# A two-block network: the mixer's projections in another order, its modulation columns made earlier and later

## The chip, the cores and the metric

One program runs on one core of one Trainium2 chip. The metric is the time of one execution on the device, in microseconds (us). The kernel before took 1466.2 us (median of three runs, 1460.26 to 1466.62).

The core has a matrix engine (PE; PEld is its loading of weights), a vector engine (DVE), an activation engine (ACT), a general engine (POOL) and SP, which here does nothing but start DMA transfers, one after the other, in the order in which they are written. Each engine takes its own instructions in order, and waits for the others by semaphores.

## The reference, cut to what matters

Two blocks run one after the other on 256 tokens of width 1024, in float32. The first has two layers of attention and mlp, the second a mixer and a mixture of 16 experts. Before each of these parts the input is normed and modulated by a shift and a scale, and its result is added through a gate. These six columns of 1024 numbers come from a conditioning vector by a matrix product of its own:

```python
mod = cond @ ada_w[layer] + ada_b[layer]                       # first block, per layer
sh1, sc1, g1, sh2, sc2, g2 = jnp.split(mod, 6, axis=-1)
...
m  = jax.nn.silu(c) @ w_mod[l] + b_mod[l]                      # second block
mc = jax.nn.silu(c_ctx) @ w_mod[l] + b_mod[l]                  # the same for its context of 256 tokens
h  = rms_norm_2(x, norm1_g[l]) * (1.0 + sc1) + sh1
hc = rms_norm_2(xc, norm1_g[l]) * (1.0 + csc1) + csh1
...
gq, gk, gv, nq, nk, nv, fu, cu, gl = jnp.split(h @ w_in, ...)  # the mixer
y_gqa = gqa_latent(q, k, v, kc, vc)                            # grouped-query attention
y_na  = neighbourhood_latent(nq, nk, nv, nkc, nvc, rpb)        # neighbourhood attention
y_fn  = fourier_mix(fu)
y_cv  = conformer_conv(cu, ...)     # a * sigmoid(b), 31 taps along the tokens, norm, silu
out   = merge_branches((y_gqa, y_na, y_fn, y_cv), gl, w_branch, w_out)
x = x + g1 * y                      # then norm, sh2, sc2, the experts, g2
```

## The kernel before

Every product of float32 matrices is made of three products of a reduced kind: a tile of 128 x 1024 weights (512 KB) is brought by DMA into `raw`; ACT casts it to `hi` (L322), DVE subtracts to get `lo` (L323), and PE multiplies hi by hi, hi by lo and lo by hi (`mm3`, L334 to L336). `raw` has four buffers, `hi` and `lo` five each. A tile of weights that DVE or ACT splits late holds PE.

The modulation columns are not made on PE. A step of `gemv_steps` brings a 512 KB tile of `adaT` into `ada` (two buffers) and has DVE multiply it by the conditioning row, which lies in a `crow` tile, and sum it into one of 48 columns of `mod` (L461). Steps are queued with `later` or `todo`, and `fill(n)` makes the next n of them wherever the program calls it. There are 128 such loads. `mod[0]` and `mod[1]` belong to the two layers of the first block, `mod[2]` to the second block; `modc` holds the first 16 columns for the context.

The order is this. The second attention, `odd`, has projections, the difference attention (scores L671, their row maximum on DVE at L673, values L1279) and, threaded into it, MoBA attention with its output projection at the end; it makes no columns. The second mlp, `mlp(1)`, goes through eight steps `c`; each has 96 matmuls of 256 columns for w1 (L1195 to L1197) and 48 of 512 for w2, and calls `fill(FILL[1][c])`: first the eight columns 40 to 48 of `mod[1]` (its own gate), then the conditioning rows of the second block (`silu_row`), and its columns 0 to 16, with two DVE instructions each since `modc` is made from the same tile. `block2_rows` is the queue of the second block.

The mixer projects the keys, values and queries of grouped-query attention; then `others()` yields step by step through the neighbourhood keys (`nkT`) and values (`nv`), the two halves of the convolution's input (`za`, `z`), the neighbourhood queries (`nqT`) and Fourier's input (`u`). The attention's loop `attend(gqa, ...)` takes a step of `others()`, `FILL_GQA` columns and `EARLY_CONV` steps of the convolution at each of its yields: scores on PE (L1465), their maximum on DVE (`nm`, L1467), the exponential on ACT, a transpose and a copy (`row`, L651), the values (L1437). A convolution is 4 x 30 taps, each one DVE instruction (L1539), plus four first ones (L1535). `attend(na, ...)` does the same for the neighbourhood attention (L1482, L1487), with `CONV` steps of the convolution and the merges of the other branches beside it. Last come `merge(1)`, the output projection and the routing to experts.

Slots (`A1`, `A2`, `O0`, `O1`) are named places in the memory; a tile that takes a slot waits until its last holder has been read. The list that each engine works through comes from a scheduler, which places instructions by its own estimates within the written order.

Of the kernel before, what the change touches and what calls it, by code (L numbers as in the profile page):

```python
# [27 lines left out]
ODD_COLS = [(512 * i, 512 * i + 512) for i in range(6)]  # L28
FILL = [[6] * 8, [4, 4, 4, 4, 4, 4, 0, 0]]
LAST_T = 4  # L30
# [7 lines left out]
NRAW = 12  # L38
CONV = 3
TAPS = 3  # L40
EARLY_CONV = 1
NATIVE = ("raw", "hi", "lo") * 4 + ("hi", "lo")
# [19 lines left out]
CONTEXT = [0] * 6 + [2, 2]  # L62
FILL_GQA = [3,2,2,1,2,2,2,1,2,2,2,2,0,2,2,0,4]
FILL_NA = []
# [17 lines left out]
def pack(w, us):  # L82
# [13 lines left out]
    + [GQ + 64 * h + d for h in range(8) for d in HALF]  # L96
    + list(range(NK, NK + 512)) + list(range(NV, NV + 512))
    + list(range(CU, CU + 1024)) + list(range(NQ, NQ + 512)) + list(range(FU, FU + 512))
    + [GL + D * n + c for n in MERGE for c in range(D)]
# [147 lines left out]
class Block:  # L247
# [900 lines left out]
    def mlp(self, l):  # L1148
# [4 lines left out]
        acc = [[self.ps(tag="pj"), self.ps(tag="pj")], [self.ps(tag="pj"), self.ps(tag="po")]]  # L1153
        self.later(l, [self.crow0], [mod], range(40, 48))
        if l == 0:
            for a, b in ((0, 16), (16, 24), (24, 40)):
                self.later(1, [self.crow0], [self.mod[1]], range(a, b))
        else:
            self.todo.append(self.block2_rows())
            context = self.context()  # L1160
# [60 lines left out]
    def block2_rows(self):  # L1221

        mod = self.mod[2]
        cc, c2 = self.silu_row(2), self.silu_row(1)
        yield from self.gemv_steps(2, [cc, c2], [self.modc, mod], range(0, 16))
        for a, b in ((16, 24), (24, 40), (40, 48)):
            yield from self.gemv_steps(2, [c2], [mod], range(a, b))

    def odd(self):
# [22 lines left out]
        def val(v):  # L1252
            def g(t, ps, w):
                nc.scalar.copy(v[:, t], ps)
            yield from self.native_steps(st, self.hf, g)
# [66 lines left out]
        def side():  # L1322
# [3 lines left out]
            yield from moba  # L1326

        for g in (qk_(("diff_q_norm", "diff_k_norm"), q1), val(v1)):
            for _ in g:
                pass  # L1330
        side = side()
        for _ in difference_whole():
            next(side, None)
        out = self.out_proj(Stream(A["odd_out"], units(D, COLS_1024, 0)), 8, oT)
        for _ in moba:
# [48 lines left out]
    def mixer(self):  # L1384
# [108 lines left out]
        nkT = self.slot("A1", [P, 4, 512])  # L1493
        nv = self.slot("A2", [P, 4, 512])
        zz = self.slot("O0", [P, 2, 4, S])
        z, za = zz[:, 0], zz[:, 1]
        u = self.slot("O1", [P, 2, 512])

        def others():

            def f(n, ps):
                nc.scalar.copy(nkT[:, n], ps)
            yield from self.proj_T(st, [h, hc], f, 1)

            def f(i, ps, w):
                nc.scalar.copy(nv[:, i], ps)
            yield from self.proj_steps(st, D, four, f)

# [11 lines left out]

            def f(n, ps):
                nc.scalar.mul(nqT[:, n], ps, 0.125)
            yield from self.proj_T(st, [h], f, 2)

            def f(t, ps, w):
                nc.scalar.copy(u[:, t], ps)
            yield from self.proj_steps(st, D, acts, f)
# [27 lines left out]
        for _ in side:  # L1555
            pass


# [79 lines left out]
        for g in (cv, side):  # L1638
            for _ in g:
                pass  # L1640
        self.fill(99)
        mT = (self.slot("A1", [P, 8, S], F32R), self.slot("A2", [P, 8, S], F32R))
        for _ in merge(1, y1):
            pass
        for i, y in enumerate((y0, y1, y2)):
# [461 lines left out]
```

## Time and profile before

| | |
|---|---|
| median of three runs | 1466.2 us |
| the profiled execution, its own time | 1464.86 us |
| its span (first to last instruction) | 1463.1 us |
| mean granted TensorE clock | 0.969 |
| PE busy | 1379.0 us, 94% |
| PEld busy | 1115.6 us, 76% |
| DVE busy | 1111.6 us, 76% |
| ACT busy | 817.0 us, 56% |

The parts that the change touches lie, in us from the span's start, at about 409 to 547 (`odd`), 547 to 760 (`mlp(1)`), 760 to 812 (first projections of the mixer), 812 to 907 (grouped-query attention with `others()`), 907 to 930 (Fourier), 930 to 1046 (neighbourhood attention with merges) and 1046 to 1105 (`merge(1)` and the output projection). The share of a busy engine over the whole span says little about one of these; each is read for itself.

### The profile page before, as it was taken

Reading aid. Unit: us, or ns where it says so; the run is one execution under the profiler, and the core shown is the slowest. Engines: PE = TensorE matmul, PEld = TensorE weight load, DVE = VectorE, ACT = ScalarE, POOL = GpSimd, SP = SyncE. Lnnn points to the kernel's source line nnn. Section 1 sums busy time; section 2 is a strip of 40 time slices with the busy share of each in tenths; the row PEclk is TensorE's granted clock in tenths of the full one; section 3 lists DMA queues with packets and bytes.
Section 4 is the critical chain, followed back from the end, with each engine's and each line's share of the span. In section 5 each row is a group of like instructions: output and inputs, shape, how many; then the busy total and the mean of one; then the engine's idle time right before and its main releaser. Section 6 shows DMA issues by size and latency. Waiting matters only on the chain.

```text
span 1463.1 us, 20532 instructions
## 1 busy us (share of the span) xinstructions
PE 1379.0 (94%) x7366; PEld 1115.6 (76%) x7366; DVE 1111.6 (76%) x1879; ACT 817.0 (56%) x1304; POOL 153.6 (11%) x189
## 2 busy tenths in 40 slices
PE   6879899999999999999999999999998899999996
PEld 4768668989854557989988897677786788888884
DVE  4779777778753666799775679997676888888986
ACT  4456455445422455545655556555545487778764
POOL 0269410000022200000003000000000000000001
PEclk9999799999999979999999999999999899999998
DMA  9657447899972222878633777444554599999993
GB/s 350 242 187 235 159 153 241 304 312 316 333 250 85 101 88 98 304 255 295 241 126 122 238 239 233 143 144 147 177 188 157 185 344 341 328 334 324 331 330 142
DMA packets 93838, 333.56 MB, mean 228 GB/s; under 512 B 10656, under 2 KB 11808, under 8 KB 93216
## 3 DMA queue, kind: packets, MB, share of 16 engines
q1 hardware_dynamic: 93728, 332.17, 66.1%
q8 instruction: 60, 0.98, 0.3%
q14 instruction: 50, 0.41, 0.1%
HBM read 331.08 MB, written 1.05 MB: 227 GB/s over the span
## 4 chain that ended last, share of the span: by engine, by line
PE 65%; DMA 12%; DVE 11%; ACT 4%; issue 4%; POOL 3%; SPq 1%; ACTq 0%; POOLq 0%; DVEq 0%
PE pj L334 6%; PE pj L335 6%; PE pj L336 6%; DMA raw<-in_w_dram 6%; PE pj L381 5%; PE ps L334 5%; PE ps L336 5%; PE ps L335 5%; DMA ada<-in_adaT_dram 4%; PE ps L411 3%; DVE ada L461 3%; DVE lo L323 2%; ACT hi L322 2%; PE ps L1197 2%; PE ps L1195 2%
## 5 line engine op out<-in xcount | busy, mean ns | idle before, releaser
L322 ACT CAST hi<-raw 128x1024 fp32r<-128x1024 f32 (+3 forms) x311 | 313.2, 1016 | 235.5 <-DMA raw<-in_w_dram 84.6
L323 DVE TENSOR_TENSOR lo<-raw,hi 128x1024 fp32r<-128x1024 f32 (+4 forms) x301 | 357.7, 1198 | 98.6 <-ACT hi L322 95.8
L461 DVE CUSTOM_DVE_ANT_0 ada<-ada,crow 128x1024 f32<-128x1024 f32 x128 | 161.6, 1272 | 30.0 <-DMA ada<-in_adaT_dram 30.0
L334 PE MATMUL pj<-hi,H 128*128 128x512 f32 (+3 forms) x312 | 117.9, 382 | 3.7 <-ACT H L814 1.8
L1197 PE MATMUL ps<-H,lo 128*128 128x256 f32 x408 | 116.9, 286 | 2.3 <-DVE lo L323 2.2
L335 PE MATMUL pj<-lo,H 128*128 128x512 f32 (+3 forms) x312 | 117.0, 376 | 0.8 <-DVE lo L323 0.6
L334 PE MATMUL pj<-hi,A 128*128 128x512 f32 (+1 forms) x293 | 115.3, 394 | 2.4 <-DVE w L960 2.4
L1195 PE MATMUL ps<-H,hi 128*128 128x256 f32 x408 | 116.8, 286 | 0.7 <-ACT hi L322 0.7
L1196 PE MATMUL ps<-H,hi 128*128 128x256 f32 x408 | 116.3, 285 | 0.0
L335 PE MATMUL pj<-lo,A 128*128 128x512 f32 (+1 forms) x293 | 114.7, 392 | 0.7 <-DVE lo L323 0.6
L336 PE MATMUL pj<-hi,H 128*128 128x512 f32 (+3 forms) x312 | 115.2, 373 | 0.0
L336 PE MATMUL pj<-hi,A 128*128 128x512 f32 (+1 forms) x293 | 114.1, 389 | 0.0
L1197 PEld LDWEIGHTS ps<-H,lo 128*128 128x128 f32 x408 | 79.0, 194 | 3.2 <-DVE lo L323 3.1
L1195 PEld LDWEIGHTS ps<-H,hi 128*128 128x128 f32 x408 | 79.0, 194 | 1.6 <-ACT hi L322 0.9
L1196 PEld LDWEIGHTS ps<-H,hi 128*128 128x128 f32 x408 | 79.0, 194 | 0.4
L334 PEld LDWEIGHTS pj<-hi,H 128*128 128x128 f32 x312 | 59.7, 192 | 17.7 <-issue 6.0
L334 PE MATMUL ps<-hi,A 128*128 128x512 f32 x180 | 71.3, 396 | 0.0
L335 PE MATMUL ps<-lo,A 128*128 128x512 f32 x180 | 70.3, 391 | 0.0
L336 PE MATMUL ps<-hi,A 128*128 128x512 f32 x180 | 70.3, 391 | 0.0
L323 DVE TENSOR_TENSOR lo<-crow,hi 128x1024 fp32r<-128x1024 f32 x52 | 62.6, 1222 | 8.8 <-ACT hi L322 7.9
L334 PEld LDWEIGHTS pj<-hi,A 128*128 128x128 f32 x293 | 55.2, 189 | 16.3 <-issue 4.4
L335 PEld LDWEIGHTS pj<-lo,H 128*128 128x128 f32 x312 | 60.2, 193 | 9.3 <-DVE lo L323 1.1
(557 smaller groups left out, 3295.2 us busy)
## 6 DMA issues: line engine op xcount, KB each, us to landing
ada<-in_adaT_dram SPq DMA_DIRECT2D x128, 512.0 KB, 4.9
raw<-in_w_dram SPq DMA_DIRECT2D x128, 512.0 KB, 5.3
raw<-in_gu_dram SPq DMA_DIRECT2D x78, 512.0 KB, 5.7
raw<-in_in_dram SPq DMA_DIRECT2D x60, 512.0 KB, 4.3
raw<-in_down_dram SPq DMA_DIRECT2D x37, 512.0 KB, 5.5
crow<-in_gu_dram SPq DMA_DIRECT2D x34, 512.0 KB, 5.8
raw<-in_even_in_dram SPq DMA_DIRECT2D x24, 384.0 KB, 4.0
crow<-in_down_dram SPq DMA_DIRECT2D x18, 512.0 KB, 5.9
```

What stands on the lines that cost most here:

```text
L322: self.nc.scalar.copy(hi, src)
L323: end = (engine or self.nc.vector).tensor_tensor(lo, src, hi, ALU.subtract)
L334: mm(ps, ah, bh, start=start, stop=False)
L335: mm(ps, ah, bl, start=False, stop=False)
L336: mm(ps, al, bh, start=False, stop=stop)
L381: self.nc.tensor.matmul(pss[t], hf[:, k, t * P:t * P + P], ws[k], start=k == 0, stop=k == 7)
L411: self.nc.tensor.transpose(out, in_, self.ident[:p, :p])
L461: nc.vector.tensor_tensor_reduce(out=o, in0=wt, in1=r, scale=1.0, scalar=0.0, op0=ALU.mult, op1=ALU.add, accum_out=m[:, j:j + 1])
L1195: mm(ps[:, n % 2], wh, hh[:, k], start=k == 0 and n % 2 == 0, stop=False)
L1196: mm(ps[:, n % 2], wh, hl[:, k], start=False, stop=False)
L1197: mm(ps[:, n % 2], wl, hh[:, k], start=False, stop=k == 7 and n % 2 == 1)
```

## The change

The convolution's two projections come first in `others()`, ahead of the neighbourhood keys and values, and the weights' columns in `IN2_ORDER` move with them. `z` and `za` take the slot A2 (before: O0), `nv` takes O0 (before: A2), allocated when its first tile is copied; its four pieces come in another order, and the first is held in PSUM until the second is there. `u` is allocated later. `EARLY_CONV` is 2 (before: 1) and `CONV` is 1 (before: 3).

The columns of the modulation move. `odd` now makes 16: `mod[1]` 40 to 48, then, after the conditioning row, `mod[2]` 16 to 24, one at a time by `FILL_ODD`. `mlp(1)` makes 32 in all eight of its steps: 0 to 16 (with `modc`) from the first step on, then 24 to 40. The grouped-query attention makes none. The last eight, 40 to 48, are made in `merge(1)` by `FILL_MERGE`. Nothing else is computed than before, and 128 tiles of `adaT` are loaded as before.

```diff
-FILL = [[6] * 8, [4, 4, 4, 4, 4, 4, 0, 0]]
+FILL = [[6] * 8, [4, 4, 4, 4, 4, 4, 4, 4]]
+FILL_ODD = [0] + [1] * 20
-CONV = 3
+CONV = 1
-EARLY_CONV = 1
+EARLY_CONV = 2
-FILL_GQA = [3,2,2,1,2,2,2,1,2,2,2,2,0,2,2,0,4]
+FILL_GQA = []
+FILL_MERGE = [1, 1, 2, 1, 1, 2]
...
-    + list(range(NK, NK + 512)) + list(range(NV, NV + 512))
-    + list(range(CU, CU + 1024)) + list(range(NQ, NQ + 512)) + list(range(FU, FU + 512))
+    + list(range(CU, CU + 1024)) + list(range(NK, NK + 512)) + list(range(NV, NV + 512))
+    + list(range(NQ, NQ + 512)) + list(range(FU, FU + 512))
...
     def block2_rows(self):
         mod = self.mod[2]
-        cc, c2 = self.silu_row(2), self.silu_row(1)
-        yield from self.gemv_steps(2, [cc, c2], [self.modc, mod], range(0, 16))
-        for a, b in ((16, 24), (24, 40), (40, 48)):
-            yield from self.gemv_steps(2, [c2], [mod], range(a, b))
+        cc = self.silu_row(2)
+        yield from self.gemv_steps(2, [cc, self.c2], [self.modc, mod], range(0, 16))
+        for a, b in ((24, 40), (40, 48)):
+            yield from self.gemv_steps(2, [self.c2], [mod], range(a, b))
+
+    def odd_rows(self):
+        yield from self.gemv_steps(1, [self.crow0], [self.mod[1]], range(40, 48))
+        self.c2 = self.silu_row(1)
+        yield from self.gemv_steps(2, [self.c2], [self.mod[2]], range(16, 24))
...
+        fills = iter(FILL_ODD)
+        self.todo.append(self.odd_rows())
         for g in (qk_(("diff_q_norm", "diff_k_norm"), q1), val(v1)):
             for _ in g:
-                pass
+                self.fill(next(fills, 0))
         side = side()
         for _ in difference_whole():
             next(side, None)
+            self.fill(next(fills, 0))
+        self.fill(99)
...
-        nv = self.slot("A2", [P, 4, 512])
-        zz = self.slot("O0", [P, 2, 4, S])
+        zz = self.slot("A2", [P, 2, 4, S])
...
+            def f(i, ps, w):
+                held.append(ps)
+                if i:
+                    if not nvs:
+                        nvs.append(self.slot("O0", [P, 4, 512]))
+                    for n in range(len(held)):
+                        nc.scalar.copy(nvs[0][:, (i - len(held) + 1 + n + 2) % 4], held[n])
+                    held.clear()
...
-        self.fill(99)
         mT = (self.slot("A1", [P, 8, S], F32R), self.slot("A2", [P, 8, S], F32R))
-        for _ in merge(1, y1):
-            pass
+        fills = iter(FILL_MERGE)
+        for _ in merge(1, y1):
+            self.fill(next(fills, 0))
+        self.fill(99)
```

The scheduler's lists of the vector engine show what becomes of it at three places. The first is the end of the first mlp, where the second attention's norm begins: `w` (L887, L889 after) takes a result of the mlp out of PSUM, `x` adds it, the rows that write `A` make the normed input, and `rs` is its factor. Before:

```order
L887 TENSOR_TENSOR w_3891<-pj_2158,row_3778 128x512
L888 TENSOR_TENSOR x_12_80<-x_12_80,w_3891 128x512
L531 TENSOR_TENSOR A_780_3900<-x_12_80,row_3793 128x512
L887 TENSOR_TENSOR w_3895<-pj_2159,row_3778 128x512
L888 TENSOR_TENSOR x_12_80<-x_12_80,w_3895 128x512
L531 TENSOR_TENSOR A_780_3900<-x_12_80,row_3793 128x512
L507 SCALAR_TENSOR_TENSOR rs_3903<-ssx_79,rs_3903 128x1
L539 SCALAR_TENSOR_TENSOR A_780_3900<-A_780_3900,rs_3903,xn_3806 128x512
```

After:

```order
L889 TENSOR_TENSOR w_3891<-pj_2158,row_3778 128x512
L890 TENSOR_TENSOR x_12_80<-x_12_80,w_3891 128x512
L533 TENSOR_TENSOR A_780_3900<-x_12_80,row_3793 128x512
L463 ISA ada_4023,mod_2_62<-ada_4023,crow_461 128x1024
L463 ISA mod_2_62 128x1
L889 TENSOR_TENSOR w_3895<-pj_2159,row_3778 128x512
L890 TENSOR_TENSOR x_12_80<-x_12_80,w_3895 128x512
L533 TENSOR_TENSOR A_780_3900<-x_12_80,row_3793 128x512
L463 ISA ada_4077,mod_2_62<-ada_4077,crow_461 128x1024
L463 ISA mod_2_62 128x1
L509 SCALAR_TENSOR_TENSOR rs_3903<-ssx_79,rs_3903 128x1
L541 SCALAR_TENSOR_TENSOR A_780_3900<-A_780_3900,rs_3903,xn_3806 128x512
```

Two modulation columns (L463, before L461) stand now ahead of `rs`.

The second place is the first step of the second mlp on the same engine, where `lo` are splits of its weights and `modc_64` the context's columns. Before:

```order
L323 TENSOR_TENSOR A_1047_5006<-ps_5007,A_1047_5006 128x4x128
L461 ISA ada_5014,mod_2_62<-ada_5014,crow_461 128x1024
L461 ISA mod_2_62 128x1
L461 ISA ada_5017,mod_2_62<-ada_5017,crow_461 128x1024
L461 ISA mod_2_62 128x1
L323 TENSOR_TENSOR lo_5169<-raw_5166,hi_5168 128x1024
L461 ISA ada_5020,mod_2_62<-ada_5020,crow_461 128x1024
L461 ISA mod_2_62 128x1
L323 TENSOR_TENSOR lo_5175<-raw_5172,hi_5174 128x1024
```

After:

```order
L325 TENSOR_TENSOR A_1065_5062<-ps_5063,A_1065_5062 128x4x128
L422 SCALAR_TENSOR_TENSOR crow_5070<-xn_5072,crow_5070 128x1024
L325 TENSOR_TENSOR lo_5239<-raw_5236,hi_5238 128x1024
L423 TENSOR_SCALAR crow_5070<-crow_5070 128x1024
L463 ISA xn_5078,modc_64<-ada_5076,crow_5070 128x1024
L463 ISA modc_64 128x1
L463 ISA ada_5076,mod_3_63<-ada_5076,crow_4357 128x1024
L463 ISA mod_3_63 128x1
L463 ISA xn_5083,modc_64<-ada_5081,crow_5070 128x1024
L463 ISA modc_64 128x1
L325 TENSOR_TENSOR A_1065_5062<-ps_5171,A_1065_5062 128x4x128
L463 ISA ada_5081,mod_3_63<-ada_5081,crow_4357 128x1024
```

Each tile of `adaT` is read twice from the first step on, and the conditioning row is made ahead of it.

The third place is the start of the grouped-query attention, again on the vector engine; `xn` is the low part of its second half of queries, `nm` the first row maximum. Before:

```order
L323 TENSOR_TENSOR lo_7472<-raw_7469,hi_7471 128x1024
L323 TENSOR_TENSOR xn_7416<-w_7157,xn_7416 128x8x64
L461 ISA ada_7442,mod_3_63<-ada_7442,crow_5462 128x1024
L461 ISA mod_3_63 128x1
L461 ISA ada_7445,mod_3_63<-ada_7445,crow_5462 128x1024
L461 ISA mod_3_63 128x1
L1467 TENSOR_REDUCE nm_7436<-ps_7433 128x1
```

After:

```order
L325 TENSOR_TENSOR lo_7571<-raw_7568,hi_7570 128x1024
L1520 SCALAR_TENSOR_TENSOR A_1443_7246<-w_7501,A_1443_7246 128x256
L1520 SCALAR_TENSOR_TENSOR A_1443_7246<-w_7504,A_1443_7246 128x256
L1560 SCALAR_TENSOR_TENSOR A_1443_7246<-A_1443_7246,cols_84 128x244
L325 TENSOR_TENSOR xn_7524<-w_7231,xn_7524 128x8x64
L1560 SCALAR_TENSOR_TENSOR A_1443_7246<-A_1443_7246,cols_84 128x245
L325 TENSOR_TENSOR lo_7863<-raw_7860,hi_7862 128x1024
L1560 SCALAR_TENSOR_TENSOR A_1443_7246<-A_1443_7246,cols_84 128x246
L1479 TENSOR_REDUCE nm_7544<-ps_7541 128x1
```

Convolution taps (L1560, before L1539) and the convolution's inputs (L1520) stand among the queries' splits and ahead of the maximum. All 120 taps lie ahead of the twelfth of the 16 maxima `nm`; before, 20 lay ahead of the fifteenth and the others behind it.

## Rows read from the trace of the kernel before

**Rows 1.** The page: engines by busy time, and the chain that ended last.

```profile
PE 1379.0 (94%) x7366; PEld 1115.6 (76%) x7366; DVE 1111.6 (76%) x1879; ACT 817.0 (56%) x1304; POOL 153.6 (11%) x189
...
PE 65%; DMA 12%; DVE 11%; ACT 4%; issue 4%; POOL 3%; SPq 1%; ACTq 0%; POOLq 0%; DVEq 0%
```

**Rows 2.** By stretch: PE, PEld, DVE, ACT, POOL busy, granted clock, DMA, GB/s.

```profile
812.00:907.00 95.00, 92.91 (x622) 79.98 (x621) 77.01 (x136) 52.23 (x93) 0.00 (x0) 1.00 0.73 244
...
930.00:1046.00 116.00, 114.93 (x564) 82.24 (x564) 97.60 (x231) 69.41 (x134) 1.86 (x2) 0.99 0.49 158
```

**Rows 3.** PE's waits from 760 to 1106: total, times, longest.

```profile
PE ps L1358 <- ACT pt L662: 1.5, 1, 1.5
PE ps L1482 <- DVE A L323: 1.1, 1, 1.1
...
PE ps L481 <- ACT row L482: 0.8, 1, 0.8
PE po L1437 <- DVE row L651: 0.6, 1, 0.6
```

**Rows 4.** PE in order of time, grouped-query attention: start, duration, what.

```profile
861.40 0.28 PE L1358 MATMUL ps<-H,hi 128*128 128x256 f32 x1
861.52 0.28 PE L1359 MATMUL ps<-H,hi 128*128 128x256 f32 x1
```

**Rows 5.** In order of time, start of the second attention, DVE and PE.

```profile
405.00 0.16 DVE L507 SCALAR_TENSOR_TENSOR rs<-ssx,rs 128x1 f32<-128x1 f32 x1
...
405.81 0.75 DVE L539 SCALAR_TENSOR_TENSOR A<-A,rs,xn 128x512 f32<-128x512 f32 x1 [0.66 <-POOL rs L508]
...
407.96 1.03 PE L411 MATMUL ps<-consts,A 128*128 128x128 f32 x8
...
409.77 1.98 PE L381 MATMUL pj<-hi,H 128*128 128x512 f32 x4 [0.77 <-ACT H L549]
```

**Rows 6.** In order of time, difference attention, DVE; then PE.

```profile
456.28 0.29 DVE L673 CUSTOM_DVE_ANT_0 sc<-ps,consts 128x128 f32<-128x128 f32 x1 [9.10 <-PE ps L671]
...
466.77 0.29 DVE L673 CUSTOM_DVE_ANT_0 sc<-ps,consts 128x128 f32<-128x128 f32 x1 [9.85 <-PE ps L671]
...
485.85 1.54 PE L1279 MATMUL po<-A,pt 128*128 128x128 f32 x6 [1.47 <-ACT pt L651]
```

**Rows 7.** Busy time by stretch, end of the second attention.

```profile
516.70:533.80 17.10, 16.53 (x54) 10.73 (x54) 9.56 (x31) 8.61 (x24) 2.41 (x4) 0.50 0.27 90
```

**Rows 8.** The tile `ada`, 540 to 1070: DVE's idle time for it, landing.

```profile
  DMA ada<-in_adaT_dram: 17.5, 19
...
DMA to landing us min/median/max: 3.2/4.8/8.5
```

**Rows 9.** Busy time by stretch in the second mlp; then PE's wait there.

```profile
600.00:620.00 20.00, 20.00 (x135) 18.54 (x134) 13.39 (x16) 9.12 (x12) 0.00 (x0) 1.00 0.90 309
620.00:640.00 20.00, 20.00 (x135) 18.54 (x134) 19.23 (x26) 11.91 (x15) 0.00 (x0) 1.00 0.71 234
...
PE ps L1197 <- DVE lo L323: 1.1, 1, 1.1
```

**Rows 10.** DVE's groups, 812 to 907; then 907 to 1046: busy, mean ns, idle.

```profile
L461 DVE CUSTOM_DVE_ANT_0 ada<-ada,crow 128x1024 f32<-128x1024 f32 x25 | 30.3, 1223 | 9.7 <-DMA ada<-in_adaT_dram 9.7
L323 DVE TENSOR_TENSOR lo<-raw,hi 128x1024 fp32r<-128x1024 f32 x20 | 24.2, 1220 | 2.1 <-ACT hi L322 2.1
L1467 DVE TENSOR_REDUCE nm<-ps 128x1 f32<-128x512 f32 x15 | 10.3, 686 | 2.3 <-PE ps L1465 2.3
...
L1539 DVE SCALAR_TENSOR_TENSOR O<-O,cols 128x251 f32<-128x251 f32 (+14 forms) x99 | 42.7, 470 | 0.0
```

**Rows 11.** In order of time, DVE: queries' low part, eight taps, `merge(1)`'s split.

```profile
810.85 0.69 DVE L323 TENSOR_TENSOR xn<-w,xn 128x512 fp32r<-128x512 f32 x1 [0.75 <-ACT xn L322]
...
920.32 3.18 DVE L1539 SCALAR_TENSOR_TENSOR O<-O,cols 128x245 f32<-128x245 f32 x8
...
1083.42 2.59 DVE L323 TENSOR_TENSOR lo<-raw,hi 128x1024 fp32r<-128x1024 f32 x2 [0.25 <-ACT hi L322]
```

More of the change, by code (lines that the diff above doesn't have):

```diff
@@ L1153, in mlp @@
         acc = [[self.ps(tag="pj"), self.ps(tag="pj")], [self.ps(tag="pj"), self.ps(tag="po")]]
-        self.later(l, [self.crow0], [mod], range(40, 48))
         if l == 0:
+            self.later(0, [self.crow0], [mod], range(40, 48))
             for a, b in ((0, 16), (16, 24), (24, 40)):
@@ L1493, in mixer @@
         nkT = self.slot("A1", [P, 4, 512])
-        nv = self.slot("A2", [P, 4, 512])
-        zz = self.slot("O0", [P, 2, 4, S])
+        zz = self.slot("A2", [P, 2, 4, S])
         z, za = zz[:, 0], zz[:, 1]
-        u = self.slot("O1", [P, 2, 512])
+        nvs, us = [], []
         def others():
[L1501 to L1507, printed above, removed]
             def f(n, ps):
@@ L1521, in f @@
             def f(n, ps):
+                nc.scalar.copy(nkT[:, n], ps)
+            yield from self.proj_T(st, [h, hc], f, 1)
+            def f(i, ps, w):
[6 more added lines that the diff above has]
+                    held.clear()
+            held = []
+            yield from self.proj_steps(st, D, four[2:] + four[:2], f)
+            def f(n, ps):
                 nc.scalar.mul(nqT[:, n], ps, 0.125)
             yield from self.proj_T(st, [h], f, 2)
+            us.append(self.slot("O1", [P, 2, 512]))
             def f(t, ps, w):
-                nc.scalar.copy(u[:, t], ps)
+                nc.scalar.copy(us[0][:, t], ps)
             yield from self.proj_steps(st, D, acts, f)
@@ L1556, in mixer @@
             pass
+        nv, u = nvs[0], us[0]
         y2, y1 = [self.slot(s, [P, 2, 4, S], F32R) for s in ("A4", "A0")]
@@ L1640, in mixer @@
                 pass
+        mT = (self.slot("A1", [P, 8, S], F32R), self.slot("A2", [P, 8, S], F32R))
+        fills = iter(FILL_MERGE)
+        for _ in merge(1, y1):
+            self.fill(next(fills, 0))
         self.fill(99)
-        mT = (self.slot("A1", [P, 8, S], F32R), self.slot("A2", [P, 8, S], F32R))
-        for _ in merge(1, y1):
-            pass
         for i, y in enumerate((y0, y1, y2)):
```

## The prediction

> **What bounds the kernel now.** I read the page first, then the busy time by stretch, then the waits of PE, then the order of time at the places where the lists change. PE is busy in 94% of the span, DVE in 76%, and the chain that ended last runs over PE for 65% and over DVE for 11% [rows 1]. By stretch it is closer still: 92.91 of 95 us in the grouped-query attention, where DVE has 77.01, and 114.93 of 116 us in the neighbourhood attention, where DVE has 97.60; the granted clock is 1.00 and 0.99, the upper of its two levels [rows 2]. "Busy" could hide gaps, since matmuls overlap. So the start-to-start time counts: two matmuls of 256 columns that follow each other start 0.12 us apart [rows 4], and the stretches with large DVE load show the same step. PE is not spaced by DVE there. What DVE costs is seen in PE's waits alone: in the mixer's 346 us the longest are 1.5 on ACT's part of a softmax, 1.1 on a split, 0.8 and 0.6 [rows 3]; in the second mlp it is one of 1.1 [rows 9].
>
> That is the first result: work that leaves DVE, or DVE's 9.7 us of waiting for `ada` in the grouped-query attention [rows 10], can give back at most these few microseconds. In the second attention the frame is another: PE works for 17.1 us at a clock of 0.50, the lower level [rows 7]; the same work would take 8.5 us less at 1.00.
>
> **Part by part.** The 128 column steps, 512 KB and 1.22 us of DVE each, stay; PE's work and the bytes stay. Only places move. Gains are written below zero.
>
> Start of the second attention. Two steps stand ahead of `rs` now, 2 x 1.22 = 2.4 us. `rs` came at 405.00, the first normed half at 405.81 + 0.75 = 406.56, and PE took it at 407.96 [rows 5]. So 1.4 us are hidden by PE's last matmuls of the mlp, and the rest, 1.0, lies on the path, as does the 0.77 that PE waits at 409.77 already. The second half is pushed by the same steps; I take +1.2, between 0 and 3.6 (three steps).
>
> Middle of the second attention. Seven steps stand among the instructions between the last rope of the keys and the second pair of scores' maxima. DVE idles 9.10 us before the first and 9.85 before the second [rows 6]. Seven steps need 8.5 us of DVE, and the loads come in pairs, since `ada` has two buffers: three rounds of 4.8 us to landing [rows 8] and the first pair loaded ahead; 14.4 + 3 x 1.22 = 18.1 us, against 18.95 of idle time. It fits, barely: 0, and up to 10.3 if each landing takes the longest 8.5 [rows 8] in place of 4.8 (11.1 more, less the 0.8 that is left). Behind the steps wait the maxima, and behind these ACT's exponential and PE's values, which wait 1.47 us already [rows 6]. The last step falls in the tail with the low clock: 0, with -8.5 as its other end, if the low stretch goes, and +1.2 if the step lies on the path there.
>
> Second mlp. In 600 to 620 DVE was busy for 13.39 of 20 us; in 620 to 640, where each tile was read twice, for 19.23, and the only wait of PE in all of the mlp was 1.1 [rows 9]. The change puts that load at the first step, where splits of the weights stand among it, and adds the making of the row ahead of it (1.9 by two instructions of the size of a split and a half). Between `ada`'s two buffers and the five of `lo` I take one more wait of the size seen, +1.1; between 0 and 4.8 (one landing on the path). Where the load was, from the third step on, half of the old wait goes: -0.5, between -1.1 and 0. The last two steps get four single columns each in a stretch with DVE time to spare: 0.
>
> Start of the grouped-query attention. Straight ahead of the second `xn` stand two inputs of the convolution, that wait for ACT's tanh, and a tap. `xn` came at 810.85 [rows 11], just ahead of the first scores. Eight taps take 3.18 us, 0.39 each [rows 11]; an input is as wide, and taken at 0.42: 2 x 0.42 + 0.39 = +1.2; between 0 and 3, the seven taps that stand there.
>
> Grouped-query attention. It loses 25 steps of 1.22 us (30.3) and 9.7 of waiting, and gets up to 99 taps (42.7 us at 470 ns) [rows 10]. The taps are bunched: after's list has, from the first maximum to the ninth, 97 taps x 0.39 = 37.8, 7 splits x 1.22 = 8.5, 11 maxima and copies x 0.69 = 7.5 [rows 10, 11], in all some 53.8 us on DVE. PE's list has there 192 matmuls of 256 columns x 0.12 = 23, 111 of 512 at twice that less a little, 25, and transposes and values, 2.4: some 50.5. DVE falls 3 us behind; a maximum has some slack before PE's transposes need it, so 2.0 reach PE. The waits of before, 1.5 and 0.6 [rows 3], go: 2.0 - 2.1 = -0.1; between -2.1 and +3. What is late next is then the split and the maximum, behind taps.
>
> The slots change holders and cost nothing: A2's last readers, matmuls of the second mlp, are done before the mixer begins. If `z` waited for one, its first copy on ACT would be late by one projection, inside the range of the next term. The neighbourhood values hold one PSUM tile until the second is there: one copy on ACT late, +0.6, between 0 and 2. Neighbourhood attention and Fourier: DVE loses the taps, and the wait of 1.1 for a split [rows 3] goes: -1.1, between -1.1 and 0. `merge(1)`: the last two steps stand ahead of the split that ran at 1083.42 [rows 11], and their loads ahead of three weight tiles on SP. Two steps and a landing, 2.4 + 4.8 = 7.2 us, are hidden by weights split ahead; the 0.8 that PE waits for `row` [rows 3] may grow: +0.3, between 0 and 2.
>
> Sum: 1.2 + 0 + 0 + 1.1 - 0.5 + 1.2 - 0.1 + 0.6 - 1.1 + 0.3 = +2.7. The profiled execution took 1464.86 us, 1.3 below the median and 4.6 above the lowest run; on its own time the sum is 1467.6. I forecast 1468.
>
> On the measure of PE the Trainium skill (Perfetto Trace Analysis, Identifying the Most-Contended Engine) speaks against me: it calls matmul busy time a bad measure of how near PE is to its limit, and wants the share of the weight loads. That leads to the second rival.
>
> **Rivals.** First, faster: the low clock of the second attention goes or shortens. For it: it begins behind a chain of small waits in the tail of the attention, and the shift of 1.2 us and the DVE steps ahead change what PE does there. Against: the change leaves these instructions as they are. Price: -8.5, and let the two costs at the attentions' starts (1.2 each) be hidden: 1467.6 - 8.5 - 2.4 = 1457. The Trainium skill (TensorE: Matmul & The Clock Gate, Part 1: The HAM clock gate) ties the clock to how busy PE has been of late, and the half level behind a thin stretch agrees with that.
>
> Second, much faster: PE has room after all. In the neighbourhood attention weights are loaded in 82.24 of 116 us [rows 2]; if DVE set the pace, its relief of 42.7 us would let the stretch shrink to that, 33.8 us: 1434. Against it stands the even step of 0.12 us [rows 4]. That is the reading which the Trainium skill's page on Perfetto Trace Analysis, in the section named above, would favour; this trace doesn't.
>
> Third, slower: the seven steps in the second attention come late. DVE takes its instructions in order, so a step that waits for its tile holds the maxima. It decides when the landing of `ada` is above some 5.1 us, with 18.95 us of room against three rounds and 3.7 of DVE. Price 10.3: 1478. For it: DVE waited for `ada` 19 times in the later stretch, 17.5 us [rows 8]. Against: DMA has more room in the second attention than there.
>
> Fourth, slower: DVE is too full. The second mlp's start at 4.8 in place of 1.1, the grouped-query start at 3 in place of 1.2, the attention at +3 in place of -0.1, the held PSUM at 2 in place of 0.6: +10 more, 1478.
>
> **How the numbers follow.** A measurement of this kernel tells some 0.5%, 7.3 us, from no change. Forecast 0.54 (its own range 1461 to 1473), first rival 0.18, second 0.03, third 0.13, fourth 0.12. Faster 0.21, same 0.54, slower 0.25. All ends at their lowest give 1452, all at their highest 1495; they don't come together, and the range goes from 1456, the first rival's, to 1479, that of the slower two.
>
> **What would show it.** Right: busy PE within 2 us of before in the neighbourhood attention though DVE falls by some 40; no new wait of PE over 2 us in the grouped-query attention, with the waits there on `nm` or `lo`; DVE's step at the second attention's start 2.4 us ahead of `rs`; scores' maxima still idle for less than 2 us behind the steps. Wrong: values L1279 waiting over 5 us; PE waiting for `lo` more than 3 us in the mlp's first two steps; a start-to-start step of matmuls below 0.12; the low clock gone from the tail.

## The result, and the profile after

The changed kernel took 1473.99 us (median of 12 runs, 1468.28 to 1484.80), the kernel before 1463.97 us in the runs beside it (12 runs, 1455.51 to 1467.82). The ratio is 1.0076, 95% interval [1.0055, 1.0098]: some 11 us slower (the medians lie 10.0 us apart), and the interval is clear of no change. The profiled execution of the changed kernel took 1468.38 us with a span of 1466.6, only 3.5 us over the span of before; that it was one of its shortest is taken up below.

By stretch of the changed kernel, with the columns of [rows 2]:

```profile
600.00:620.00 20.00, 19.60 (x132) 18.05 (x131) 19.30 (x28) 8.66 (x11) 0.00 (x0) 1.00 0.88 297
...
812.00:907.00 95.00, 92.59 (x615) 79.62 (x614) 83.03 (x174) 50.72 (x88) 0.00 (x0) 1.00 0.34 105
930.00:1046.00 116.00, 116.00 (x548) 83.03 (x547) 70.54 (x158) 67.48 (x131) 1.86 (x2) 0.99 0.46 147
```

The work went where the lists said. DVE lost 27 us in the neighbourhood attention (97.60 to 70.54, where the prediction had some 40), and PE's idle time there shrank by 1; against [rows 2], that is what "off the path" looks like. DVE is at 19.30 of 20 us in 600 to 620, where it was at 13.39 [rows 9].

PE's longest waits in the changed kernel from 760 to 1106, to be held against [rows 3]:

```profile
PE pj L336 <- ACT hi L324: 2.4, 1, 2.4
PE ps L413 <- DVE O L1638: 1.4, 2, 0.8
PE ps L413 <- DVE w L325: 0.9, 2, 0.5
```

The waits on the softmax (1.5 and 0.6) and on the split (1.1) are gone, as forecast; new is one of 2.4 for a cast by ACT ahead of the first scores, and 1.4 at `merge(1)`. (The wait of 0.8 for `row` is still there, 0.5, just past the end of this window.)

In the second mlp there are three waits, where there was one of 1.1 [rows 9]:

```profile
PE ps L1197 <- DVE w L581: 1.1, 1, 1.1
PE ps L483 <- ACT row L484: 0.7, 1, 0.7
PE ps L1199 <- DVE lo L325: 0.4, 1, 0.4
```

The larger changes are in the second attention. Its start in the changed kernel, in order of time, where [rows 5] had `rs` at 405.00 and one wait of 0.77:

```profile
399.99 1.22 DVE L463 CUSTOM_DVE_ANT_0 ada<-ada,crow 128x1024 f32<-128x1024 f32 x1 [1.21 <-DMA ada<-in_adaT_dram]
...
403.26 1.22 DVE L463 CUSTOM_DVE_ANT_0 ada<-ada,crow 128x1024 f32<-128x1024 f32 x1
...
404.40 0.15 DVE L509 SCALAR_TENSOR_TENSOR rs<-ssx,rs 128x1 f32<-128x1 f32 x1
...
406.11 0.63 PE L413 MATMUL ps<-consts,A 128*128 128x128 f32 x4 [2.03 <-DVE A L541]
...
407.91 2.08 PE L383 MATMUL pj<-hi,H 128*128 128x512 f32 x2 [1.17 <-ACT H L551]
```

DVE first waits 1.21 us for the tile and then does the two steps ahead of `rs`; PE waits 2.03 and 1.17 in place of 0.77. Behind that the clock falls to its lower level of 1.2 GHz (0.5 of the full 2.4), as the stretches 407 to 414 and, for the tail, 519 to 524 and 524 to 539 show (granted clock third from the end):

```profile
519.00:524.00 5.00, 4.95 (x20) 3.46 (x20) 1.97 (x9) 3.18 (x10) 0.00 (x0) 0.66 0.01 4
524.00:539.00 15.00, 11.63 (x61) 6.74 (x60) 11.83 (x40) 9.05 (x27) 2.41 (x4) 1.00 0.40 140
407.00:414.00 7.00, 6.09 (x11) 2.94 (x11) 5.33 (x15) 1.93 (x7) 1.00 (x2) 0.51 1.02 391
```

So in this execution the low clock of the tail [rows 7] was nearly gone (519.8 to 523.2 is left of 17.1 us), and 7 us of it came up at the start, where the kernel before had a stretch just ahead, 393.8 to 397.3. In the tail at full clock PE is busy for 11.63 of 15 us: it waits for DVE and ACT, the longest for DVE's last product of the difference attention's output (1.53).

And the middle of the second attention, DVE, ACT and PE of the changed kernel in order of time, up to the first values, which waited 1.47 in [rows 6]:

```profile
468.04 0.29 DVE L675 CUSTOM_DVE_ANT_0 sc<-ps,consts 128x128 f32<-128x128 f32 x1 [0.77 <-PE ps L673]
...
469.83 1.04 ACT L324 CAST hi<-raw 128x1024 fp32r<-128x1024 f32 x1 [10.14 <-DMA raw<-in_odd_out_dram]
...
471.26 0.40 ACT L664 ACTIVATE sc<-sc,nm 128x128 f32<-128x128 f32 x1
...
487.03 1.04 ACT L324 CAST hi<-raw 128x1024 fp32r<-128x1024 f32 x1 [4.16 <-DMA raw<-in_odd_out_dram]
487.98 0.58 ACT L653 COPY A<-ps 128x512 f32<-128x512 f32 x1
...
488.93 0.49 ACT L653 COPY pt<-ps 128x384 f32<-128x384 f32 x1
...
489.48 1.65 PE L1287 MATMUL po<-A,pt 128*128 128x128 f32 x6 [3.83 <-ACT pt L653]
```

The second pair of maxima on DVE is not late (it still waits for PE, 0.77). The first pair, at 458.37, comes straight behind a step and some 0.8 us late, but ACT idles for 10.14 us soon after its exponential, so that costs nothing. ACT is what is late: it has the cast of a tile of the output projection's weights ahead of the exponential in its order, and waits for that tile. In the kernel before the same cast ran 3.5 us sooner:

```profile
466.31 1.05 ACT L322 CAST hi<-raw 128x1024 fp32r<-128x1024 f32 x1 [8.72 <-DMA raw<-in_odd_out_dram]
```

SP shows why, first the changed kernel, then the one before (start, time from the first to the last issue of a run, what, how many):

```profile
451.17 13.24 SPq L448 DMA_DIRECT2D ada<-in_adaT_dram  x6
464.50 0.38 SPq L311 DMA_DIRECT2D raw<-in_odd_out_dram  x1
467.30 0.33 SPq L448 DMA_DIRECT2D ada<-in_adaT_dram  x1
472.16 22.62 SPq L311 DMA_DIRECT2D raw<-in_odd_out_dram  x6
```

```profile
446.43 0.33 SPq L309 DMA_DIRECT2D hi<-in_odd_in_dram  x1
462.48 28.92 SPq L309 DMA_DIRECT2D raw<-in_odd_out_dram  x7
```

Six loads of `adaT`, each waiting for one of two buffers, stand ahead of the first such tile, and one more ahead of the second. The first goes out 2.0 us later (464.50 for 462.48), but 1.27 of these are the delay that the whole attention has by then (the second maxima come at 468.04 for 466.77); 0.75 are the queue's. The larger part is the transfer: with two loads of `adaT` under way the tile took 5.25 us to land, for 3.76 before. Together the cast is 2.25 us late against the maxima. Each later tile waits for a buffer that a split frees, so the delay stays, and the values wait 2.36 us more.

### The profile page after: what moved, and what is told of

It is laid out like the page before. It is cut to its first block, busy times and chain, and to the rows that moved or that the text cites. A ratio compares the mean times of both kernels' runs of the same rounds, so it can differ in the third digit from the quotient of the medians.

```text
span 1466.6 us, 20551 instructions
## 1 busy us (share of the span) xinstructions
PE 1374.3 (94%) x7366; PEld 1109.6 (76%) x7366; DVE 1114.4 (76%) x1879; ACT 817.3 (56%) x1304; POOL 154.5 (11%) x189
## 4 chain that ended last, share of the span: by engine, by line
PE 62%; DMA 12%; DVE 12%; ACT 5%; POOL 4%; issue 4%; SPq 0%; ACTq 0%; POOLq 0%; DVEq 0%
DMA raw<-in_w_dram 6%; PE pj L336 6%; PE pj L338 6%; PE pj L337 6%; PE ps L336 5%; PE ps L338 5%; PE ps L337 5%; PE pj L383 3%; DMA ada<-in_adaT_dram 3%; PE ps L413 3%; DVE ada L463 3%; DVE lo L325 2%; ACT hi L324 2%; POOL hr L502 2%; PE po L1449 2%
## 5 line engine op out<-in xcount | busy, mean ns | idle before, releaser
L463 DVE CUSTOM_DVE_ANT_0 ada<-ada,crow 128x1024 f32<-128x1024 f32 x128 | 161.6, 1272 | 31.7 <-DMA ada<-in_adaT_dram 31.5
```

Of the source, the lines that this page charges most:

```text
L463: nc.vector.tensor_tensor_reduce(out=o, in0=wt, in1=r, scale=1.0, scalar=0.0, op0=ALU.mult, op1=ALU.add, accum_out=m[:, j:j + 1])
```

## The experiments

Ratios are against the kernel before, run beside each on the same chip, with 95% intervals.

**e1: the changed kernel again.**

> The changed kernel once more, for a second trace of it and its spread. Theory A (the change itself adds some 8 to 11 us of waits of PE, and the profiled execution, 3.5 us longer in its span, was a short one because its second attention had less time at the lower clock): 8 to 12 us slower than the kernel before, and a trace with more time at a granted clock of 0.5 than the 36 us (lost clock, 1 minus the granted clock summed over the span) of the first one. Theory B (the first trace is typical): 3 to 4 us slower, the same places at the lower clock.

1.009 [1.0062, 1.0117], 1470.04 against 1458.16 us. PE's longest waits in its second attention:

```profile
PE po L1287 <- ACT pt L653: 5.3, 2, 5.0
PE ps L413 <- DVE A L541: 3.1, 1, 3.1
PE ps L413 <- DVE sm L1108: 1.8, 1, 1.8
PE pj L383 <- ACT H L551: 0.7, 1, 0.7
PE pj L336 <- ACT O L324: 0.7, 1, 0.7
```

The waits are the same ones; the two at the start come to 3.8 us for 3.2, and the first values wait 5.0 for 3.8. Its granted clock, summed as 1 minus the clock over the whole span, lost 43.5 us, the first trace's 38.2. Theory A holds for these two traces; but the kernel before lost 44.8 in its first trace and 50.2 in e5, so that the sum of lost clock is no measure of the loss. Of the span, 1469.1, more below. e1 had the low clock in 406 to 413, 487 to 495 and 522 to 533, each behind one of these waits. The last two are not new: the kernel before has a stretch behind its first values, of half that length (486.0 to 489.4), and the one in the tail, behind the same 1.8 us on `sm`.

**e2: the mixer's part alone.** `FILL`, `FILL_GQA`, `block2_rows`, `odd` and the last `fill(99)` as before; all else of the change.

> Only the mixer's part of the change: the convolution's projections first, slots, EARLY_CONV 2 and CONV 1; all modulation columns where they were before. Theory A (the loss is in the columns that moved): within 3 us of before, with PE's waits in the grouped-query attention as before or up to 3 us longer, since DVE now has the columns and the taps there. Theory C (the loss is in the mixer, where DVE gets too full): 6 us slower or more.

1.0027 [0.9998, 1.0055]. PE's waits on the copy `row` in the grouped-query attention grew from 0.6 to 2.4 us (three times), and the new 2.4 ahead of the first scores is there:

```profile
PE pj L336 <- ACT hi L324: 2.4, 1, 2.4
PE po L1448 <- DVE row L653: 2.4, 3, 1.3
PE ps L413 <- DVE w L325: 0.9, 2, 0.5
```

Theory A's "within 3 us" is just missed (5.5 us between the medians, 0.27% by the ratio, some 4 us), theory C's 6 not reached; the interval takes in zero.

**e3: the columns' part alone.** The mixer as before.

> Only the columns' part: 16 in the second attention, 32 in the second mlp, 8 in the last merge, none in the grouped-query attention; the mixer's order as before. Theory A: 7 to 11 us slower. Theory C: within 3 us, or faster by the 2 us of waits that leave the grouped-query attention.

1.0078 [1.0049, 1.0107]: all of the loss by itself. Theory A.

**e4: only the 16 columns in the second attention.**

```diff
-FILL = [[6] * 8, [4, 4, 4, 4, 4, 4, 0, 0]]
+FILL = [[6] * 8, [0, 0, 4, 4, 4, 4, 0, 0]]
+FILL_ODD = [0] + [1] * 20
-FILL_GQA = [3,2,2,1,2,2,2,1,2,2,2,2,0,2,2,0,4]
+FILL_GQA = [2,1,1,1,1,2,1,1,1,2,1,2,0,1,2,0,4]
...
```

with `odd_rows` and its calls in `odd` as in the change.

> Only the 16 columns in the second attention; the columns 0 to 16 of the second block stay in the third to sixth step of the second mlp, and 24 to 48 in the grouped-query attention, as before. Theory A with the second attention as its place (two steps ahead of its norm, PE idle 3.6 in place of 1.0 us there, a fall to the lower clock behind it, 2.3 us more at the first values): 6 to 10 us slower, most of e3. If the second mlp is the place (its first steps): within 2 us of before, and e3 slow.

1.0035 [1.0010, 1.0060], some 5 us: the second attention is a place of loss, but not "most of e3". In the second mlp from 600 to 760 e4 shows no wait of PE at all, while e3 shows

```profile
PE ps L483 <- ACT row L484: 1.4, 1, 1.4
PE ps L1197 <- DVE w L581: 1.0, 1, 1.0
PE ps L1199 <- DVE lo L325: 0.6, 1, 0.6
```

**e5: the kernel before again.**

> The kernel before, once more, for a second trace. If its first trace was typical: about 43 us of lost clock, 17 us of the second attention's tail at a clock of 0.5, and PE's wait of 1.5 us for the first values (L1279) of the difference attention. If that low stretch comes and goes from execution to execution, it is absent or shorter here, and the waits are the same.

Span 1463.5 us at a clock of 0.966, the same 17 us at the lower clock in the tail (516.5 to 533.6), the first values waiting 1.5. So that stretch was there in both traces of this kernel; whether it is in every execution these two can't say. This one took 1465.26 us, while the timed runs of the same kernel on that chip had a median of 1459.86 and a mean clock of 0.971. The first trace of before (1464.86) is nearer to its median, 1463.97.

**e6 and e7: is it the loads or DVE's steps?** In e6 the columns 16 to 24 are all made from one loaded tile; in e7 they are loaded and multiplied over 16 of 1024 elements (`in0=wt[:, :16]`).

> The changed kernel, but the eight columns mod[2] 16 to 24 in the second attention are all made from one tile (seven loads of 512 KB are left out, so these columns are wrong); DVE still does eight steps of 1.22 us there, seven of them ahead of the first scores. Theory D (the loads stand ahead of the output projection's weight tiles on SP and delay them; ACT casts such a tile ahead of the softmax's exponential, so PE's first values come late): PE's wait for the first values falls from 4 to 5 us to 1.5 to 2, time 3 to 4 us below the changed kernel, some 6 to 9 above before. Theory E (DVE's steps hold the maxima of the scores): the wait stays at 4 to 5 us, time as the changed kernel's.

> The changed kernel, with all loads, but the same eight steps multiply 16 of 1024 elements each (0.1 us of DVE in place of 1.22; these columns are wrong). Theory D: the wait for the first values stays at 4 us or more, or shrinks by 1 to 2 us since buffers come free earlier. Theory E: it falls to 1.5 to 2 us.

The wait for the first values, e6 first, then e7:

```profile
PE po L1291 <- ACT pt L653: 2.3, 2, 2.0
```

```profile
PE po L1287 <- ACT pt L653: 5.8, 3, 5.2
```

With DVE's steps and no loads it is 2.0, with the loads and hardly any steps 5.2: theory D. The time of e7 is of no use: the wrong gate sends the tokens to experts otherwise, and the expert stage runs twice as long (643 us for 322; 1797 us in all). In e6 that stage took as long as in the others (323 us). e6 came out at 1.0087 [1.0053, 1.0121], not below the changed kernel as expected. In its trace the first values do come 4.3 us sooner, counted from the end of the first mlp, but the low clock of the tail lasted 20.5 us (515.8 to 536.3) and took that back (table below). So the wait's cause is shown, and what it is worth in the whole time is not.

**e8: no step ahead of the norm.**

> The changed kernel with FILL_ODD = [0, 0, 0, 0, 2, 2] + [1] * 20: the same 16 columns in the second attention, but no step ahead of its norm. If the two steps ahead of rs, and the loads ahead of the projection's weights, make the loss there: PE's two waits at the start (3.6 to 4.3 us) fall to about 1, the fall to the lower clock behind them goes, and the time is 3 to 6 us below the changed kernel. If the start costs nothing in the end (PE waits later instead): no difference. The wait for the first values stays at 4 to 5 us in either case.

The two waits became one of 0.8 us, as before the change, and the fall of the clock behind them went (the stretch just ahead, now 391.4 to 394.8, is back, as in the kernel before):

```profile
PE po L1287 <- ACT pt L653: 5.0, 2, 4.7
PE ps L413 <- DVE sm L1108: 1.8, 1, 1.8
PE pj L383 <- ACT H L551: 0.8, 1, 0.8
```

The time did not move: 1.0083 [1.0054, 1.0111]. The first values came 1.9 us sooner than in the changed kernel, counted from the end of the first mlp, but here too the tail was long at the lower clock, 0.53 over 22 us:

```profile
517.00:539.00 22.00, 20.76 (x67) 13.35 (x66) 14.11 (x45) 10.66 (x30) 2.41 (x4) 0.53 0.33 120
```

**e9: e3 without columns in the last four steps of the mlp.** `FILL[1] = [4, 4, 4, 4, 0, 0, 0, 0]`, `FILL_GQA = [1] * 16`.

> e3 (columns alone) with nothing in the last four steps of the second mlp: FILL[1] = [4, 4, 4, 4, 0, 0, 0, 0], and the columns 24 to 40 in the grouped-query attention, one at each step. If the last four steps of the mlp are where e3 loses beyond e4 (PE's waits there of 1.2 on the context's norm and 1.0 to 1.5 on the rows before the mixer): these two waits go, and the time is 2 to 4 us below e3, 0.5 to 0.65% above before. If the doubled columns at the mlp's start are the place: as e3, 0.78%.

1.0058 [1.0030, 1.0087], where the first theory has it; the two waits are gone from the trace, the one on `lo` (0.9) stays, and the second mlp takes 2.3 us less than in e3 (199.6 us for 201.9). The interval overlaps that of e3, so the 0.2% are likely, not shown.

**e10 and e12: eight columns in the second attention, placed out of the way.** The kernel before with

```diff
+FILL_ODD = [0, 0, 0, 0, 2, 2, 1, 1, 1, 1]
-FILL_GQA = [3,2,2,1,2,2,2,1,2,2,2,2,0,2,2,0,4]
+FILL_GQA = [2,1,1,1,1,2,1,1,1,2,1,2,0,1,2,0,4]
...
+    def odd_rows(self):
+        yield from self.gemv_steps(1, [self.crow0], [self.mod[1]], range(40, 48))
```

and the columns 16 to 24 of `mod[2]` in the first two steps of the second mlp, in place of those eight.

> The kernel before with only eight columns in the second attention, none ahead of its norm and all loaded ahead of the output projection's weights (FILL_ODD = [0, 0, 0, 0, 2, 2, 1, 1, 1, 1]); the second mlp has as many columns as before in each step, and the grouped-query attention eight fewer. If the two waits (start, first values) are what the second attention's columns cost in e4: both are as in the kernel before, 0.35% of e4 goes, and the 2 us of waits in the grouped-query attention shrink: between 0 and 3 us faster than before (ratio 0.998 to 1.000). If columns in the second attention cost by something else (traffic, the lower clock): 0.2% slower or more.

> e10 once more, to settle its sign. If its gain is real (the waits of 1.5 and 0.6 us in the grouped-query attention are gone, and the second attention as before): 1 to 3 us faster than before, ratio 0.998 to 0.999, and the two runs together below 1. If e10 was chance: between 0.999 and 1.002.

0.9985 [0.9963, 1.0007] and 0.9984 [0.9964, 1.0004]. Against e4 that is 0.5% (7 us; by the intervals 3 to 12) less, with eight columns fewer in the second attention and the same number in the grouped-query attention. Number and place changed together, so these runs don't tell which of the two counts. PE's waits of e12 from 400 to 1100 begin

```profile
PE po L1287 <- ACT pt L653: 1.8, 2, 1.5
PE ps L413 <- DVE sm L1108: 1.8, 1, 1.8
PE ps L413 <- DVE A L541: 1.7, 2, 1.2
PE ps L413 <- DVE w L325: 0.9, 2, 0.5
PE ps L336 <- ACT H L553: 0.8, 1, 0.8
PE pj L383 <- ACT H L551: 0.8, 1, 0.8
```

The start (0.8) and the first values (1.5) are as before, and the waits of 1.5 and 0.6 in the grouped-query attention [rows 3] are gone (one on the exponential is there instead, 1.0 in e10 and 0.3 in e12). Each interval just takes in 1. Taken as two independent measurements of the same ratio, half a width of 0.0021 divided by the root of two is 0.0015: 0.9985, from 0.997 to 1.000, probably 2 us faster than before. That it is faster than the changed kernel is shown: the intervals of the two lie nearly 0.5% apart.

**e11: only the order of the projections and the slots.** e2 with `CONV = 3`, `EARLY_CONV = 1`.

> e2 (the mixer alone) with EARLY_CONV 1 and CONV 3 as before: only the order of the projections and the slots differ from before. If the order costs (the new wait of 2.6 us for a cast ahead of the first scores): 0.2 to 0.3% slower, as e2, with that wait. If the taps crowded into the grouped-query attention cost: the longer waits for the copy of the softmax (L653, 2.9 us in e2) go, and the time is within 0.1% of before.

1.0003 [0.9975, 1.0030]. Neither theory as put: the time is that of the second, but the waits on `row` are still there (2.3 us), as is the one of 2.4 ahead of the scores. The wait on the softmax that PE had at that place before, 1.5, is gone, which may pay for it. e2 and e11 overlap; whether the taps crowded into the grouped-query attention cost something stays open.

## Why the prediction was right and wrong

The range, 1456 to 1479, held the time and the forecast of 1468 lies 6 us below it. But the forecast's change was +2.7 us and the measured one is 10. The likeliest case, no change, did not come: the loss is past 0.5%, on the side that had a chance of 0.25. That the range held is in part luck: its upper end came from two slower rivals, and neither came by the mechanism that it named. Of the signs named in advance, the right ones on busy PE and on the scores' maxima came; against them a new wait of over 2 us (2.4) stands at the grouped-query attention, the values waited 3.8 us in the first trace and 5.0 in e1, where over 5 was to mean wrong, and the low clock of the tail was nearly gone in the first trace. What bounds the kernel was read rightly, and the parts then fall so:

- **DVE's relief gives back only PE's few microseconds.** Right. PE's waits for the softmax and the split went (3.2 us), and nothing else followed from 27 us less of DVE in the neighbourhood attention. No wait came of the held PSUM tile (+0.6). The rival that PE has room after all (1434) is refuted.
- **Start of the second attention, +1.2.** Right in time, and short of what follows. PE waits 2.4 us more in the first trace (2.03 + 1.17 for 0.77), 3.0 more in e1 (3.1 + 0.7): the term left out that DVE would first wait for the tile (1.21). But in both traces PE also came sooner, since the low stretch that the kernel before has at 393.8 to 397.3 was missing. In e3, which has it, PE waits 1.1 more, and from the end of the first mlp to the first projection all take about as long (20.1 us before, 20.7 and 19.9 in the changed kernel, 20.9 in e3). What the sum had at nothing is the fall of the clock behind these waits: 6.0 us of the projections ran at half clock in the first trace, and the way from the first projection to the first values grew by 5.5 us, 2.4 by the values' wait and 3.1 by that. e8 took the waits and the fall away.
- **Middle of the second attention, 0.** This is the step that failed. The 0 was worked out from DVE alone ("a step that waits for its tile holds the maxima"): three rounds of loads in 18.95 us of idle time, which was right but for 0.8 us at the first pair. What the loads do to other transfers was not followed. The output projection's weights were sent behind them and landed more slowly beside them, ACT's cast of these stood ahead of the softmax, and PE waited 2.4 to 3.5 us more. e6 and e7 tell DVE's steps and the loads apart. The third rival had the right place and the wrong engine. The last step, in the tail, was at 0 too: in all seven traces that have it at its full length PE waits 0.7 us for `O`, whose split stands behind it on DVE, and in e7, where it takes 0.2 us, that wait is missing.
- **Second mlp, +1.1 - 0.5.** The start is a wait of 0.4 to 0.9, somewhat less than taken, and the old wait of 1.1 went (in e5, without any change, it is 0.3). The four columns each in the last two steps, which I put at nothing because DVE had time to spare there, are where two waits came up, of 0.7 to 1.4 and 1.0 to 1.1: busy time by stretch said that there was room, but the context's norm on DVE and the rows on ACT now came just too late. e9, without columns in the last four steps, has neither, and e4 had none.
- **Start of the grouped-query attention, +1.2.** The size is right: from the end of the second mlp to the first scores it takes 64.7 to 65.0 us in all traces with the new order of the mixer, for 63.4 to 63.8 without. The wait that PE shows, 2.4, is another than the one I named: ACT's cast of weights, which comes behind the convolution's tanh and the queries' cast. `xn` on DVE, behind two inputs and a tap, is ready at the same time (814.74), so the two can't be told apart here:

```profile
813.43 1.08 ACT L324 CAST hi<-raw 128x1024 fp32r<-128x1024 f32 x1
...
814.06 0.68 DVE L325 TENSOR_TENSOR xn<-w,xn 128x512 fp32r<-128x512 f32 x1
...
814.56 0.50 PE L336 MATMUL pj<-hi,O 128*128 128x512 f32 x1 [2.40 <-ACT hi L324]
...
814.90 1.03 PE L413 MATMUL ps<-consts,xn 128*128 128x128 f32 x8
```

- **The taps crowded on DVE, -0.1.** Right, in the changed kernel: no wait on a maximum or on `row`. The 0.39 us for a tap was low, since 99 taps in 42.7 us [rows 10] are 0.43 each, and the changed kernel has 113 in 46.3 us there, 0.41; DVE had the slack for that too.
- **Merges, +0.3.** 1.4 at two places in the first trace, and the wait for `row` went from 0.8 to 0.5: +1.1. e10 and e11, without columns there, don't have the 1.4.
- **The low clock, rival one.** It did go from the tail in the first trace, and gave 2.6 us, not 8.5: 519.2 to 537.6 (first to last of the same two instructions) became 522.9 to 538.7. That is not the price of the low clock alone, since the last step and a wait of 1.5 stand in that stretch. In e2 and e11, where the second attention is as in the kernel before, the same stretch took 15.86 us with 9 us at the lower clock, for 18.35 with 14.6: 2.5 us for 5.6, nearly the half that I had taken. Below that, waits for DVE and ACT take over, as the 11.63 of 15 us show. The Trainium skill (TensorE: Matmul & The Clock Gate, Part 1: The HAM clock gate) ties the clock to how busy PE has been of late; that the falls stand behind PE's waits agrees with it. The price has to be read from the stretch.

The time by stage shows where the loss sits, in us from one PE instruction to another in each trace:

| from, to | before | e5 | changed | e1 | e6 | e8 | e10 | e12 |
|---|---|---|---|---|---|---|---|---|
| end of the first mlp (its gate's transposes), first projection of `odd` | 20.1 | 20.1 | 20.7 | 19.9 | 20.7 | 20.6 | 20.3 | 20.0 |
| to the first values | 76.1 | 76.1 | 81.6 | 82.2 | 77.3 | 79.7 | 76.7 | 76.2 |
| to the transposes of `mod` ahead of the second mlp | 63.3 | 63.3 | 60.5 | 62.1 | 65.3 | 65.5 | 63.3 | 63.2 |
| of these at the lower clock | 20.5 | 20.5 | 6.4 | 14.9 | 23.9 | 24.0 | 20.5 | 20.5 |
| to the last ones at its end | 199.9 | 199.2 | 201.0 | 201.9 | 201.4 | 200.7 | 198.3 | 198.4 |
| to the first scores of the mixer | 63.5 | 63.5 | 64.7 | 64.7 | 65.0 | 64.7 | 63.5 | 63.4 |
| to the transposes of `mod` behind `merge(1)` | 286.7 | 288.3 | 288.0 | 287.9 | 287.6 | 287.8 | 285.2 | 283.1 |

Over these stages the changed kernel is 7 us slower in its first trace and 9 in e1; the routing behind them gives back 0.5 and 1.1, and the experts take 322 to 323 us in all of these. Ahead of them nothing is changed, but the first trace of the changed kernel had come to the end of the first mlp 2.4 us sooner (387.24 for 389.68), and that is why its span was only 3.5 us longer. Over all traces that point lies between 383.3 and 391.6 us. The medians lie 10 us apart. Why the tail has less of the low clock in the changed kernel than before, and more in e6 and e8, so that what these two gain up to the first values is lost there, stays open. The runs without a profile can't show it; their mean clock, 0.970 for the changed kernel and 0.971 to 0.972 for the one before on the chips that show it, says that the clock is no more than a part.

By parts, from the runs: the second attention's placing some 7 us (e4 against e10 and e12; 3.6 to 4.6 by that stage in their traces), the last steps of the mlp some 3 (e3 against e9; 2.3 by the stage, and not shown by the medians), the mixer's part 0 to 8 with 4 the likeliest (e2), against some 2 us that the relieved grouped-query attention gives. What single waits are worth in the whole time is not shown: neither e6 nor e8 came out faster than the changed kernel.

## What to carry to other kernels

Work that is moved into an engine's idle time brings its loads along: follow them through the issuing queue to whatever stands behind them there or is under way beside them, to the engine that uses that, and to what that engine has queued behind it. A DVE with 19 us of idle time took seven steps of 1.22 us and held nothing that PE needed, and PE still waited 2.4 us more, for a weight tile that was sent 0.75 us later and took 1.5 us longer to land. And a stretch with room on average is not free for work ahead of an instruction that PE needs now. Eight columns whose loads are all out well ahead of the next weights cost nothing, sixteen spread evenly cost 5 us. Last, where single executions differ by as much as the terms of the sum, compare traces stage by stage, from one instruction to the same one, and not by their spans.

## What the runs showed of the hardware

A 512 KB tile landed in 3.7 to 3.8 us when no other load was just ahead of it, and in 5.1 to 6.3 us with loads of `adaT` under way (the first tile of the output projection's weights, seven traces of either kind).

The granted clock fell to 0.5 behind short waits of PE: behind 2.0 and 1.2 us at the start of the second attention, and behind 3.8 to 5.3 us at the first values. It did not fall behind 0.77 at that start in the kernel before, nor behind 1.2 without a longer wait ahead of it in e6 and e9, and behind 1.5 us at the first values it fell in both traces of the kernel before and not in e2, e11 and e12; what decides there is not shown. Where such a stretch lies and how long it is differs between executions of one kernel (the tail: 3.4 us in one trace of the changed kernel, 10.3 in the other), and so does the time up to the first changed place (383.3 to 391.6 us), so that the span of a single trace of this kernel can mislead by some 6 us, more than most terms of a sum like this one. Where PE hardly waits, the lower level costs about half of the time spent at it (3.1 us for 6.0 in the projections, 2.5 for 5.6 in the tail); it costs less once PE waits for other engines at full clock.
